# Gate-weight rounds of an mLSTM block moved from the end of the projections to their start, second slabs between first slabs, and another order of the modulation

## The chip, the cores and the metric

One NeuronCore of a Trainium2 chip. The metric is device time of one execution in microseconds. TensorE (PE) does matmuls, VectorE (DVE) and ScalarE (ACT) elementwise work, GpSimd (POOL) some more of it; SyncE (SP) issues all DMAs from one queue.

## The reference

One layer over 1024 latent tokens (width 1024) and 256 context tokens, all in fp32, cut to what matters:

```python
mod = silu(c) @ w_ada + b_ada                      # six sections of 1024: shift, scale, gate, twice
px = modulate(rms_norm(x, g_pre_mix), sh_m, sc_m) @ w_in     # and pc for the context with c_ctx
aq, ak, av, mq, mk, mv, mo, mg = split(px)         # attention q k v, mLSTM q k v o, 16 gate columns
att = window_attention(rope(aq), rope(ak), av, context keys and values, sink)   # 8 heads, 2 kv heads
mq, mk = silu(depthwise_conv3(mq, mk))
h = mlstm(mq, mk, mv, gates, forward) + mlstm(..., backward)   # state begun on the context
#   d[t,s] = b[t] - b[s] + i[s] for s <= t (backward: s >= t), else -inf;  b = cumsum(log_sigmoid(f))
#   weights exp(d - m_t) on the scores; decayed state added; divided by max(|den|, exp(-m_t))
ml = rms_norm(h) * g_mlstm_out * sigmoid(mo)
x = x + gt_m * rms_norm(concat(att, ml) @ w_out, g_post_mix)
x = x + gt_f * rms_norm(swiglu(modulate(rms_norm(x, g_pre_ffn), sh_f, sc_f)), g_post_ffn)
```

## The kernel before

Each fp32 product is made of three matmuls: operands are split in a high and a low part (`hh`, `hl` for tokens of the latent, `ch`, `cl` for the context; `w1h`, `w1l` and so on for weights), and high x high, high x low and low x high are summed in PSUM. Tokens go in tiles of 128: tiles 0 to 7 are latent, 8 and 9 context.

**The front.** The modulation comes in four quarters q (each two of eight blocks of the width): `pr_mm` multiplies by the weights, `mod_row` copies the row to SBUF, `mod_t` turns it into columns, and `mod_col` adds four partial sums and the bias. In the same quarters the first three tiles are projected as soon as a quarter is there (`sq(i, q)`, two PSUM slabs: the first of 272 columns with the 16 gates, attention values and one head of mLSTM values; the second of 384 columns with three more heads of values). `h_ts`, `h_hi`, `h_lo` modulate a tile's quarter and split it (DVE, ACT, DVE). `warm(n)` issues n matmuls on ones. Tiles 3 to 9 are prepared whole (`prep_c`: square and root on ACT, reciprocal on DVE, scaling on POOL; `prep_t`: transposes; `prep_m`, `prep_b`: modulation and split), and then get a first slab, `s1(i)`, and a second slab, `s2(i)`.

**Gates.** `gates()` needs all first slabs. It is a chain between DVE, ACT and PE: `pg` (cumulative sums), a running maximum, `pr`, a scan over chunks, `pm`, then `a_d` and `w_d` stored to DRAM, `pgt` transposed into `ucol`, and `pd`. Next, `ml_weights(n)` for each block n of 128 tokens makes the mLSTM's decay weights: for each direction d a broadcast load of `a_d` into a 128 x 512 buffer w (256 KB), four adds of a column of `ucol` and a mask (`mF` or `mB`) on DVE (L648), one exponential on ACT (L649), and a store of both directions to `w_dr[n]` (L650). I call one n a round.

**Projections.** The rest of the input projection is done by weight tiles, 13 of them (mk0 mk1 ak mq0 mq1 aq0 to aq3 mo0 to mo3), each against all tokens (`tproj`, L706 to L709); `tload` loads and splits the next weights. mk and mq go through `conv` (copies from PSUM, three DVE steps, Silu at L728). Between them lie `ada_rest` (the later sections of the modulation, on DVE), the state recursion of the mLSTM, and its queries. Of the rounds, 0 to 3 come right after the gates, 4 and 5 in mo0, 6 in mo1, 7 in mo2.

**Attention and mLSTM** follow as 16 items (block n, head group g): scores on PE (L880, L881), sums and minima on DVE (L882), exponentials on ACT (L891), scaling on POOL (L896), transposes (L1145), output (L1163). For each block the mLSTM loads the weights of its round from `w_dr` into `wl` (L903) and its queries into `qz` (L915; for blocks 0 and 1 POOL clears the tile first, L909), and PE multiplies them with state and values (L1061, L1065). The first two items' scores are already issued in mo3. `qz` of block 1 lies in buffer R8, which `ml_weights(4)` to `ml_weights(7)` use too.

The Tile scheduler sets each engine's order from its own estimates of when things are ready, except for instructions that are pinned (`pin`, the order of the program) or tied (`issue_after`). An engine works its instructions in order; SP's DMA issues too.

Of the kernel before, what the change touches and what calls it, by code (L numbers as in the profile page):

```python
# [16 lines left out]
P = 128  # L17
# [27 lines left out]
def body(tc, x, ctx, xtr, vecs, bcv, bada, gqm, gqf, wada, wmod, wsq, wt, wout, wfi, wfo,  # L45
# [134 lines left out]
    wraw = [vf[:, 1504 + 1312 * i:1504 + 1312 * (i + 1)] for i in range(2)]  # L180
# [49 lines left out]
    def prep_t(i, keep=False, parts=(0, 1)):  # L230

        xt = xts[i]
        if i >= XT:
            pts[i] = pa.tile([P, 4, P], F32, name="pt", tag="tp", bufs=2)[:, 0]
            pe.matmul(pts[i], st[:, 10 + i:11 + i].broadcast_to([P, P]), ident, start=True, stop=True)
            return
# [51 lines left out]
    def wq_load(q):  # L288
        return dma(wraw[q % 2], wsq[q])
# [17 lines left out]
    def mod_row(q):  # L307
        pin(act.copy(rr[:, 0:256], prs_[q][:, 0:256]))
        pin(dve.tensor_copy(rr[:, 256:512], prs_[q][:, 256:512]))

    pcl = {}

    def mod_t(q):
        pcl[q] = pa.tile([P, 4, P], F32, name=f"pcol{q}", tag="gx" if q < 1 else "tp", bufs=2)
        for k in range(4):
            pin(pe.transpose(pcl[q][:, k, :], rr[:, k * P:(k + 1) * P], ident))

    def mod_col(q):
# [4 lines left out]
        for g in range(4):  # L323
            pin(dve.tensor_tensor(o, pv_[:, g, :, 0:2], t, ADD))
            t = o
# [36 lines left out]
    def sq(i, q, mid=None):  # L362
# [9 lines left out]
        for n, (w, o, lo_) in enumerate(x_):  # L372
            if mid and n == 3:
# [8 lines left out]
    dve.tensor_scalar(bb[:, 1], bcol(1), 1.0, None, ADD)  # L382
    ld("x0 m00 m01 m02 m03 x1 w0 x2 m10 m11 m12 m13 w1")
# [23 lines left out]
    ld("w2")  # L407
# [51 lines left out]
    for i in (1, 2):  # L459
        h_ts(i, 2)  # L460
        h_hi(i, 2)
        h_lo(i, 2)
    pr_mm(3, 0)
    pr_mm(3, 1)
    prep_c(3, (0,))
    mod_row(3)
    prep_c(3, (1,))
    sq(1, 2, lambda: mod_t(3))
# [4 lines left out]
    h_hi(0, 3)  # L473
    w_lo(3, 0)
    h_lo(0, 3)
    w_lo(3, 1)
# [47 lines left out]
    def s2(i, bs=(0, 1)):  # L524

        if 0 in bs:
            s2ps[i] = pa.tile([P, 512], F32, name="slab", tag="mm", bufs=4)
        for b in bs:
            for k in range(4):
                mm3(s2ps[i][:, :384], hop(i, 4 * b + k), (w2h[b][:, k], w2l[b][:, k]), 4 * b + k == 0, 4 * b + k == 7)  # L530
        if 1 in bs:
            act.copy(vrow(i)[:, 1:4, 0:128], s2ps.pop(i)[:, 0:384].rearrange("p (h v) -> p h v", v=128))

# [6 lines left out]
    for i in range(ET):  # L540
        sqe = sq(i, 3)
# [5 lines left out]
        if i == 1:  # L547
# [15 lines left out]


    def gates():
# [11 lines left out]
        for d in range(2):  # L577
            f = G[:, 2 * d + 1].rearrange("p s h -> p (s h)")
            dve.scalar_tensor_tensor(lf[:, d * 64:d * 64 + 64], f, 0.0, tm[:, d * 64:d * 64 + 64], MIN, SUB)
        pg = pa.tile([P, 2, P], F32, name="pg", tag="gx", bufs=2)  # L580
        for d in range(2):
            r = slice(d * 64, d * 64 + 64)
            pe.matmul(pg[r, 0, :], lf[:, r], lw if d else up, start=True, stop=True)
            pe.matmul(pg[r, 1, :], G[:, 2 * d].rearrange("p s h -> p (s h)"), ident, start=True, stop=True)
# [12 lines left out]
        for i, t in enumerate((b, cm)):  # L597
            dve.tensor_copy(bl[0:64, i:i + 1], t[0:64, 127:128])
            dve.tensor_copy(bl[64:128, i:i + 1], t[64:128, 0:1])
        pr = pa.tile([1, 2, P], F32, name="pr", tag="gx", bufs=2)  # L600
        for i in range(2):
            pe.matmul(pr[0:1, i], bl[:, i:i + 1], ident, start=True, stop=True)
        pool.memset(mr, 0.0)
        dve.tensor_copy(rr.rearrange("p i d s h -> p i (d s h)"), pr)
        for d in range(2):
            for h in range(4):
                dve.tensor_tensor_scan(mr[:, d, 1:11, h], rr[:, 1, d, 0:10, h], rr[:, 0, d, 0:10, h], 0.0, MAX, ADD)
        pm = pa.tile([P, 1], F32, name="pm", tag="gx", bufs=2)
        pe.matmul(pm, mr.rearrange("p d s h -> p (d s h)"), one[0:1, 0:1], start=True, stop=True)
# [29 lines left out]

    def ml_weights(n):  # L640

        wt_ = R((6, 7, 8, 15)[n] if n < 4 else 8, f"w{n}", (2, 4, P))
        for d in range(2):
            s_, r0 = rows_of(n, d)
            w = wt_[:, d]
            dma(w, bcast(a_d[r0:r0 + 4, :].rearrange("(o h) t -> o (h t)", o=1)).rearrange("p (h t) -> p h t", h=4))
            for h in range(4):
                dve.scalar_tensor_tensor(w[:, h], w[:, h], ucol[:, r0 + h:r0 + h + 1], mB if d else mF, ADD, ADD)  # L648
            act.activation(w, w, AF.Exp)  # L649
# [1492 lines left out]
```

## Time and profile before

| | |
|---|---|
| median of 3 runs | 1198.51 us (1197.49 to 1199.38) |
| the profiled execution | 1199.53 us, span 1197.8 us |
| mean granted TensorE clock | 0.988 |
| TensorE busy | 1156.4 us, 97% of the span |
| VectorE, ScalarE, GpSimd busy | 776.5, 555.6, 152.0 us |

The page cuts the span into 40 slices of 30 us, and its PE row is in tenths of a slice:

```profile
PE   9989999997589999999999999999999999999997
PEclk9999999998889999999999999999999999999999
```

All slices but a few are full. The dip in slices 11 and 12 (counted from 1, 300 to 360 us, with the clock's 8s from 270 on) is where the projections hand over to attention.

### The profile page before, as it was taken

To read this page: it belongs to the slowest core of one execution; us is meant where nothing else is said; L and a number is where in the kernel's file an instruction comes from. 1 tells how busy PE (TensorE), PEld (TensorE's weight loads), DVE (VectorE), ACT (ScalarE), POOL (GpSimd) and SP (SyncE) were. 2 spreads that over 40 slices of the span, in tenths; PEclk is the share of its full clock that TensorE was granted. 3 is DMA by queue.
4 is the path that set the end of the run, shared out by engine and by line. 5 is a ranking of instruction groups with operands and counts; after the bars stand their busy time and mean duration, and the time that the engine had idled before them with its cause. 6 is when DMAs were issued, how large, how long until landed. Compare 5 with 4: busy or idle time off the path is not lost.

```text
span 1197.8 us, 16313 instructions
## 1 busy us (share of the span) xinstructions
PE 1156.4 (97%) x5901; PEld 952.3 (80%) x5901; DVE 776.5 (65%) x1417; ACT 555.6 (46%) x1035; POOL 152.0 (13%) x200
## 2 busy tenths in 40 slices
PE   9989999997589999999999999999999999999997
PEld 7889888786477876788788888888888888888886
DVE  4774758943766762458777678676777656544566
ACT  4553342223757883687534333333333435434443
POOL 1330012163335561000000000000000000000000
PEclk9999999998889999999999999999999999999999
DMA  9623736576749531421233565656543557665853
GB/s 373 256 71 94 301 106 211 160 219 204 222 145 277 177 77 58 172 87 71 62 123 132 202 219 202 213 218 237 202 167 124 197 184 260 202 216 188 298 195 123
DMA packets 102984, 216.99 MB, mean 181 GB/s; under 512 B 10228, under 2 KB 39540, under 8 KB 101496
## 3 DMA queue, kind: packets, MB, share of 16 engines
q1 hardware_dynamic: 102904, 215.95, 53.8%
q8 instruction: 46, 0.75, 0.3%
q14 instruction: 34, 0.28, 0.1%
HBM read 159.29 MB, written 55.97 MB: 180 GB/s over the span
## 4 chain that ended last, share of the span: by engine, by line
PE 82%; DVE 7%; DMA 4%; ACT 2%; SPq 2%; POOL 1%; issue 1%; DVEq 0%; ACTq 0%; POOLq 0%
PE xv L79 8%; PE xv L78 8%; PE xv L77 8%; PE pt L78 6%; PE pt L79 6%; PE pt L77 6%; PE pt L1163 2%; PE pt L1145 2%; PE op L79 2%; PE op L78 2%; PE op L77 2%; PE fx L77 2%; PE fx L79 2%; PE fx L78 2%; PE slab L378 2%; PE t L707 2%
## 5 line engine op out<-in xcount | busy, mean ns | idle before, releaser
L66 DVE TENSOR_TENSOR fo<-fr,fo 128x1024 fp32r<-128x1024 f32 x77 | 92.8, 1222 | 72.6 <-ACT fo L65 72.6
L65 ACT CAST fo<-fr 128x1024 fp32r<-128x1024 f32 x77 | 79.6, 1051 | 74.0 <-PE pt L79 34.8
L706 PE MATMUL t<-hh,th 128*128 128x512 f32 x208 | 82.3, 396 | 0.0
L707 PE MATMUL t<-hl,th 128*128 128x512 f32 x208 | 81.6, 392 | 0.0
L1545 ACT CAST wS<-wr 128x512 fp32r<-128x512 f32 x88 | 54.2, 623 | 55.2 <-PE pt L79 36.6
L1547 DVE TENSOR_TENSOR wS<-wr,wS 128x512 fp32r<-128x512 f32 x88 | 60.3, 688 | 19.8 <-ACT wS L1545 19.7
L77 PE MATMUL xv<-tT,wS 128*128 128x512 f32 x168 | 65.6, 390 | 0.0
L79 PE MATMUL xv<-tT,wS 128*128 128x512 f32 x168 | 65.6, 391 | 0.0
L78 PE MATMUL xv<-tT,wS 128*128 128x512 f32 x168 | 65.5, 390 | 0.0
L709 PE MATMUL t<-hh,tl 128*128 128x512 f32 x208 | 65.5, 394 | 0.0
L880 PE MATMUL s<-k,qh 128*128 128x256 f32 (+1 forms) x128 | 44.0, 352 | 10.3 <-DVE sm L882 7.5
L79 PE MATMUL op<-woh,ml 128*128 128x512 f32 x128 | 50.1, 391 | 1.3 <-DVE ml L66 1.3
L77 PE MATMUL op<-woh,mh 128*128 128x512 f32 x128 | 50.9, 398 | 0.0
L78 PE MATMUL op<-wol,mh 128*128 128x512 f32 x128 | 50.0, 390 | 0.0
L1293 DVE TENSOR_TENSOR wr<-wr 128x512 f32<-128x512 f32 x66 | 45.5, 690 | 1.4
L706 PEld LDWEIGHTS t<-hh,th 128*128 128x128 f32 x208 | 39.1, 188 | 8.3 <-issue 0.3
L707 PEld LDWEIGHTS t<-hl,th 128*128 128x128 f32 x208 | 39.1, 188 | 7.7 <-issue 0.7
L1579 ACT ACTIVATE es<-es 128x512 f32<-128x512 f32 x22 | 13.9, 633 | 66.5 <-DVE es L1296 66.5
L709 PEld LDWEIGHTS t<-hh,tl 128*128 128x128 f32 x208 | 37.4, 188 | 6.9 <-issue 0.7
L77 PE MATMUL pt<-fo 128*128 128x512 f32 x110 | 42.8, 389 | 0.0
L78 PE MATMUL pt<-fo 128*128 128x512 f32 x110 | 42.8, 389 | 0.0
L79 PE MATMUL pt<-fo 128*128 128x512 f32 x110 | 42.8, 389 | 0.0
(794 smaller groups left out, 3314.0 us busy)
## 6 DMA issues: line engine op xcount, KB each, us to landing
wr<-in_wfi SPq DMA_DIRECT2D x44, 512.0 KB, 4.7
wb<-in_wada SPq DMA_DIRECT2D x24, 512.0 KB, 5.9
s_d<-a SPq DMA_DIRECT2D x22, 512.0 KB, 6.5
bt<-in_wfo SPq DMA_DIRECT2D x44, 256.0 KB, 3.7
tb_d<-bt SPq DMA_DIRECT2D x11, 1024.0 KB, 3.9
fr<-s_d SPq DMA_DIRECT2D x44, 256.0 KB, 4.5
fr<-tb_d SPq DMA_DIRECT2D x44, 256.0 KB, 4.8
fr<-a_d SPq DMA_DIRECT2D x33, 256.0 KB, 4.5
```

Of the source, the lines that this page charges most:

```text
L65: act.copy(hi, raw)
L66: dve.tensor_tensor(lo, raw, hi.bitcast(F32), SUB)
L77: pe.matmul(ps, a[0], b[0], start=first, stop=False, **kw)
L78: pe.matmul(ps, a[0], b[1], start=False, stop=False, **kw)
L79: pe.matmul(ps, a[1], b[0], start=False, stop=last, **kw)
L706: pe.matmul(o, wh[:, kt], m[0], start=f, stop=False)
L707: pe.matmul(o, wh[:, kt], m[1], start=False, stop=False)
L709: pe.matmul(o, wl[:, kt], m[0], start=False, stop=l)
L880: pe.matmul(o, qh[:, h, :], k2[g][:, kc], start=True, stop=False)
L1293: dve.tensor_tensor(out, a, b, SUB)
L1545: act.copy(w[:, 0], raw)
L1547: dve.tensor_tensor(w[:, 1], raw, w[:, 0].bitcast(F32), SUB)
```

## The change

What it does:

- **Modulation.** Three raw weight buffers instead of two. For quarters 0 and 1 the four partial sums are added by a matmul with a selecting matrix (`sel2`) instead of transposes and three more adds. `mod_row` is one copy on ACT instead of halves on ACT and DVE. Loads are queued earlier, warming is 3 + 6 instead of 2 + 8, and steps of the quarters change places: `h_ts(0, 0)` ahead of the scaling of tile 1, the modulation of tile 3 behind the last quarter of tile 1.
- **Slabs.** All slab matmuls are pinned. Behind each first slab `s1(i)` from tile 3 to 8 stands half a second slab, with the transposes of tile i + 2. The activation table for exponential and logarithm is loaded ahead of the gates. The first projection weights are loaded one tile before the last.
- **Gates.** The chain is a generator, and its matmuls are pinned between pieces of the remaining second slabs: in the string of the diff, 605 is tile 6, k-tiles 0 to 5; g is the next step of the chain; t loads the second weights.
- **Rounds.** All eight rounds come right behind the gates, in eight buffer uses of R8, 15, 6, 4, 5, 7, 6, 5. For d = 1 in rounds 1, 3, 5, 6, 7 the mask is added by POOL over 128 x 512, and `ucol` goes in as the bias of four exponentials of 128 x 128 on ACT. The Silu in `conv` may issue only after the last exponential, and `ada_rest`'s first loads only after the last load of a round. In mo0 to mo2 no round is left.

```diff
-    wraw = [vf[:, 1504 + 1312 * i:1504 + 1312 * (i + 1)] for i in range(2)]
+    wraw = [vf[:, 192 + 1312 * i:192 + 1312 * (i + 1)] for i in range(3)]
+    sel2 = st[:, 52:54]
...
     def mod_row(q):
-        pin(act.copy(rr[:, 0:256], prs_[q][:, 0:256]))
-        pin(dve.tensor_copy(rr[:, 256:512], prs_[q][:, 256:512]))
+        pin(act.copy(rr, prs_[q]))
...
+    SUMQ = (0, 1)
...
         for k in range(4):
-            pin(pe.transpose(pcl[q][:, k, :], rr[:, k * P:(k + 1) * P], ident))
+            rk = rr[:, k * P:(k + 1) * P]
+            pin(pe.matmul(pcl[q][:, k, 0:2], rk, sel2, start=True, stop=True) if q in SUMQ else pe.transpose(pcl[q][:, k, :], rk, ident))
...
-        for g in range(4):
+        for g in range(1 if q in SUMQ else 4):
             pin(dve.tensor_tensor(o, pv_[:, g, :, 0:2], t, ADD))
...
-    warm(2)
+    warm(3)
     mod_t(0)
     prep_c(1, (0,))
     mod_col(0)
+    warm(6)
+    h_ts(0, 0)
     prep_c(1, (1,))
-    warm(8)
-    h_ts(0, 0)
...
-    ld("w2")
+    ld("w2 m30 m31 m32 m33 w3 x3 x4")
...
+    def pm3(ps, a, b, first, last):
+
+        for i, j in ((0, 0), (0, 1), (1, 0)):
+            pin(pe.matmul(ps, a[i], b[j], start=first and not i + j, stop=last and i == 1))
...
+        if i + 3 == NI:
+            pin(act.preload_act_table_set("natural_log_exp_and_others"))
         if i + 1 < NI:
             prep_b(i + 1)
-        with tc.issue_after(sqe) if i < ET + 2 else ExitStack():
-            s1(i)
-            if i < ET + 2:
-                s2(ET, (i - ET,))
+        s1(i)
+        if i < NI - 1:
+            s2(ET + (i - ET) // 2, range(4 * ((i - ET) % 2), 4 * ((i - ET) % 2) + 4))
+            if ET + 2 <= i + 2 < NI:
+                prep_t(i + 2, True)
...
+        if i == NI - 2:
+            tload(0)
...
+    wlast, elast = [None], [None]
+
     def ml_weights(n):
 
-        wt_ = R((6, 7, 8, 15)[n] if n < 4 else 8, f"w{n}", (2, 4, P))
+        wt_ = R((8, 15, 6, 4, 5, 7, 6, 5)[n], f"w{n}", (2, 4, P))
         for d in range(2):
             s_, r0 = rows_of(n, d)
             w = wt_[:, d]
-            dma(w, bcast(a_d[r0:r0 + 4, :].rearrange("(o h) t -> o (h t)", o=1)).rearrange("p (h t) -> p h t", h=4))
+            wlast[0] = dma(w, bcast(a_d[r0:r0 + 4, :].rearrange("(o h) t -> o (h t)", o=1)).rearrange("p (h t) -> p h t", h=4))
+            if d and n in (1, 3, 5, 6, 7):
+                pool.tensor_tensor(w, w, mB.rearrange("p (o t) -> p o t", o=1).broadcast_to([P, 4, P]), ADD)
+                for h in range(4):
+                    elast[0] = act.activation(w[:, h], w[:, h], AF.Exp, bias=ucol[:, r0 + h:r0 + h + 1]).ins
+                continue
             for h in range(4):
                 dve.scalar_tensor_tensor(w[:, h], w[:, h], ucol[:, r0 + h:r0 + h + 1], mB if d else mF, ADD, ADD)
-            act.activation(w, w, AF.Exp)
+            elast[0] = act.activation(w, w, AF.Exp).ins
         dma(w_dr[n], wt_.rearrange("p d h t -> p (d h t)"))
...
-    gates()
-    for i in range(NFILL, NI):
-        if i > ET:
-            s2(i)
-        if i in (NFILL + 1, NFILL + 2):
-            tload(i - NFILL - 1)
-        if NFILL < i < NFILL + 5:
-            ml_weights(i - NFILL - 1)
+    gt = gates()
+    next(gt)
+    for k in "605 g t 667 707 g 803 g 847 901 g 923 g 947".split():
+        if k == "g":
+            next(gt, None)
+        elif k == "t":
+            tload(1)
+        else:
+            s2(int(k[0]), range(int(k[1]), int(k[2]) + 1))
+    for n in range(NT):
+        ml_weights(n)
...
-            act.activation(d, t, AF.Silu)
+            with tc.issue_after(elast[0]):
+                act.activation(d, t, AF.Silu)
...
-        with tc.issue_after(twd[j].ins):
+        with tc.issue_after((twd[j] if acc_n.append(sec) or len(acc_n) > 1 else wlast[0]).ins):
...
-        for n in {"mo0": (4, 5), "mo1": (6,), "mo2": (7,)}.get(name, ()):
-            ml_weights(n)
```

How the order of the engines moves at three places. First the handover on DVE, where the first items' sums stand (`sm<-s`, the scores in PSUM). Before:

```order
L823 SCALAR_TENSOR_TENSOR cs_2539<-cs_2539,decb,pu 128x129 x4
L882 ISA pr__2690,sm<-s,mask,bcr 128x512
L882 ISA sm 128x1
L882 ISA pr__2690,sm<-s,mask,bcr 128x512
L882 ISA sm 128x1
L648 SCALAR_TENSOR_TENSOR w_2434<-w_2434,ucol,mF 128x128 x4
L648 SCALAR_TENSOR_TENSOR w_2434<-w_2434,ucol,mB 128x128 x4
L882 ISA pr__2690,sm<-s,mask,bcr 128x512
L882 ISA sm 128x1
```

And now:

```order
L846 SCALAR_TENSOR_TENSOR cs_2560<-cs_2560,decb,pu 128x129 x4
L905 ISA pr__2683,sm<-s,mask,bcr 128x512
L905 ISA sm 128x1
L905 ISA pr__2683,sm<-s,mask,bcr 128x512
L905 ISA sm 128x1
L905 ISA pr__2683,sm<-s,mask,bcr 128x512
L905 ISA sm 128x1
```

A round stood between the second and the third sum of item 0; the four sums now follow each other. Second, the handover on SP (`aq_dh`, `aq_dl` are the attention queries' two parts). Before:

```order
L650 DMA w_dr_980<-w_2562 128x1024
L920 DMA hs_2838<-so_d 128x4x128
L920 DMA hs_2977<-so_d 128x4x128
L903 DMA wl_3126<-w_dr_976 128x1024
L903 DMA wl_3290<-w_dr_977 128x1024
L646 DMA w_2659<-a_d 128x512 x2
L835 DMA qh<-aq_dh 64x4x128 x2
L835 DMA ql<-aq_dl 64x4x128 x2
L650 DMA w_dr_981<-w_2659 128x1024
L915 DMA qz_2968<-q_dr 64x2x128 x7
```

And now:

```order
L926 DMA wl_2672<-w_dr_1025 128x1024
L926 DMA wl_2959<-w_dr_1026 128x1024
L1010 DMA so_d<-so 128x1024
L938 DMA qz_2961<-q_dr 64x2x128 x4
L858 DMA qh<-aq_dh 64x4x128 x2
L858 DMA ql<-aq_dl 64x4x128 x2
L858 DMA qh<-aq_dh 64x4x128 x2
L858 DMA ql<-aq_dl 64x4x128 x2
L1133 DMA wor_3007<-in_wout 128x1024
L938 DMA qz_2674<-q_dr 64x2x128 x4
```

Before, the load of block 1's qz came in one piece behind the last round's store; now four of its loads stand ahead of the queries of later items, with no store of a round near them. Third, ACT where the first convolutions are (mk). Before:

```order
L649 ACTIVATE w_1207<-w_1207 128x512 x2
L65 CAST th_1391<-tw_1393 128x1024
L723 COPY cr<-t_0_1297 128x512
L723 COPY cr<-t_1_1298 128x512
L728 ACT_TABLE_LOAD
L728 ACTIVATE mk_1285<-ct 128x1024
```

And now:

```order
L65 CAST th_1440<-tw_1442 128x1024
L745 COPY cr<-t_0_1346 128x512
L745 COPY cr<-t_1_1347 128x512
L742 COPY cr<-tc_1348 128x256
L65 CAST th_1540<-tw_1542 128x1024
L677 ACTIVATE w_1294<-w_1294 128x512
L673 ACTIVATE w_1294<-w_1294,ucol 128x128 x4
L677 ACTIVATE w_1308<-w_1308 128x512
L673 ACTIVATE w_1308<-w_1308,ucol 128x128 x4
L751 ACT_TABLE_LOAD
L751 ACTIVATE mk_1334<-ct 128x1024
```

The exponentials of the last two rounds (`w_1294`, `w_1308`) stand between the copies of the first projection out of PSUM and its Silu.

More of the change, by code (lines that the diff above doesn't have):

```diff
@@ L234, in prep_t @@
             pts[i] = pa.tile([P, 4, P], F32, name="pt", tag="tp", bufs=2)[:, 0]
-            pe.matmul(pts[i], st[:, 10 + i:11 + i].broadcast_to([P, P]), ident, start=True, stop=True)
+            pin(pe.matmul(pts[i], st[:, 10 + i:11 + i].broadcast_to([P, P]), ident, start=True, stop=True))
             return
@@ L372, in sq @@
         for n, (w, o, lo_) in enumerate(x_):
-            if mid and n == 3:
+            if mid and n == at:
                 mid()
@@ L382, in body, with h_all @@
     dve.tensor_scalar(bb[:, 1], bcol(1), 1.0, None, ADD)
+    for k in range(1, 4):
+        dve.tensor_tensor(sel2, sel2 if k > 1 else ident[:, 0:2], ident[:, 32 * k:32 * k + 2], ADD)
+    def h_all(i, q):
+        h_ts(i, q)
+        h_hi(i, q)
+        h_lo(i, q)
     ld("x0 m00 m01 m02 m03 x1 w0 x2 m10 m11 m12 m13 w1")
@@ L458, in body @@
     sq(0, 2)
[L459 to L462, printed above, removed]
+    h_all(1, 2)
     pr_mm(3, 0)
+    h_all(2, 2)
     pr_mm(3, 1)
+    mod_row(3)
+    sq(1, 2, lambda: mod_t(3), 2)
     prep_c(3, (0,))
-    mod_row(3)
-    prep_c(3, (1,))
-    sq(1, 2, lambda: mod_t(3))
     w_hi(3, 0)
@@ L473, in body @@
     h_hi(0, 3)
+    prep_c(3, (1,))
     w_lo(3, 0)
+    w_lo(3, 1)
     h_lo(0, 3)
-    w_lo(3, 1)
     pool.memset(V[:, :, :, 128:129], 1.0)
@@ L522, in body, with s2, tload @@
     s2ps = {}
-    def s2(i, bs=(0, 1)):
-        if 0 in bs:
+    def s2(i, ks):
+        if 0 in ks:
             s2ps[i] = pa.tile([P, 512], F32, name="slab", tag="mm", bufs=4)
[L528 to L531, printed above, removed]
+        for k in ks:
+            pm3(s2ps[i][:, :384], hop(i, k), (w2h[k // 4][:, k % 4], w2l[k // 4][:, k % 4]), k == 0, k == 7)
+        if 7 in ks:
             act.copy(vrow(i)[:, 1:4, 0:128], s2ps.pop(i)[:, 0:384].rearrange("p (h v) -> p h v", v=128))
+    twd, tws = {}, {}
+    def tload(j):
+        wh = R(9 + j % 2, f"th{j}", (KT, P), F32R)
+        wl = R(11 + j % 2, f"tl{j}", (KT, P), F32R)
+        with tc.issue_after(xd[NI - 1].ins):
+            twd[j] = load_split(wh, wl, wt[j], R(13 + j % 2, f"tw{j}", (KT, P)))
+        tws[j] = wh, wl
     chain(lambda: dma(bcr, bcast(bcv)))
@@ L599, in gates @@
             dve.tensor_copy(bl[64:128, i:i + 1], t[64:128, 0:1])
+        yield
         pr = pa.tile([1, 2, P], F32, name="pr", tag="gx", bufs=2)
         for i in range(2):
-            pe.matmul(pr[0:1, i], bl[:, i:i + 1], ident, start=True, stop=True)
+            pin(pe.matmul(pr[0:1, i], bl[:, i:i + 1], ident, start=True, stop=True))
         pool.memset(mr, 0.0)
@@ L607, in gates @@
                 dve.tensor_tensor_scan(mr[:, d, 1:11, h], rr[:, 1, d, 0:10, h], rr[:, 0, d, 0:10, h], 0.0, MAX, ADD)
+        yield
         pm = pa.tile([P, 1], F32, name="pm", tag="gx", bufs=2)
-        pe.matmul(pm, mr.rearrange("p d s h -> p (d s h)"), one[0:1, 0:1], start=True, stop=True)
+        pin(pe.matmul(pm, mr.rearrange("p d s h -> p (d s h)"), one[0:1, 0:1], start=True, stop=True))
         mc, c1, dc = m[:, 0:1], m[:, 1:2], m[:, 2:3]
@@ L628, in gates @@
         dve.tensor_scalar(di, ind, dc, None, MUL)
+        yield
         pd = pa.tile([P, 64], F32, name="pd", tag="gx", bufs=2)
-        pe.matmul(pd, sel, di, start=True, stop=True)
+        pin(pe.matmul(pd, sel, di, start=True, stop=True))
         dve.tensor_copy(decb, pd)
```

59 lines of the change are left out of this document (22 added, 37 removed).

## The prediction

> **What bounds the kernel now.** I read the page first: the busy times and the chain that ended last.
>
> ```profile
> PE 1156.4 (97%) x5901; PEld 952.3 (80%) x5901; DVE 776.5 (65%) x1417; ACT 555.6 (46%) x1035; POOL 152.0 (13%) x200
> PE 82%; DVE 7%; DMA 4%; ACT 2%; SPq 2%; POOL 1%; issue 1%; DVEq 0%; ACTq 0%; POOLq 0%
> ```
>
> TensorE is the bound, and this change adds or removes hardly a matmul. So it can win only where PE stands still or runs slowly. I therefore took PE's waits over two stretches that the change touches: the handover from the projections to attention (285 to 345 us), and the front (0 to 112 us).
>
> ```profile
> PE pt L1061 <- DMA qz<-q_dr: 8.9, 1, 8.9
> PE s L880 <- DVE sm L882: 7.0, 4, 5.0
> PE s L880 <- DVE wl L1052: 2.6, 3, 1.9
> PE pt L1145 <- POOL pr__2854 L896: 2.1, 1, 2.1
> PE s L1047 <- ACT so L978: 1.9, 1, 1.9
> PE pt L1145 <- ACT ts__3021 L1150: 1.0, 1, 1.0
> PE pt L1061 <- ACT ts__2868 L1150: 0.7, 1, 0.7
> ...
> PE slab L378 <- ACT hh L355: 2.9, 3, 1.3
> PE pt L235 <- DVE st L220: 1.8, 2, 0.9
> PE slab L79 <- DVE hl L274: 0.9, 1, 0.9
> ```
>
> The columns are total, times and longest. The handover's seven add up to 24.2 us. Next, the windows (length, busy PE, PEld, DVE, ACT, POOL, granted clock, DMA share, GB/s):
>
> ```profile
> 120.00:180.00 60.00, 60.00 (x315) 50.50 (x314) 39.69 (x54) 22.84 (x34) 5.06 (x13) 1.00 0.54 202
> 285.00:300.00 15.00, 8.04 (x42) 6.98 (x40) 7.73 (x28) 6.73 (x17) 6.31 (x5) 0.66 0.66 183
> 300.00:320.00 20.00, 13.34 (x94) 11.13 (x93) 16.98 (x58) 17.55 (x37) 7.98 (x11) 0.99 0.82 244
> 320.00:340.00 20.00, 9.16 (x42) 6.50 (x41) 7.85 (x23) 8.60 (x18) 4.91 (x10) 0.58 0.38 110
> ```
>
> Between front and handover PE never rests (60.00 of 60.00), so what the front gains is carried to the handover unchanged, and nothing there can be gained by other engines. In the handover the clock falls to 0.66 and 0.58 in the windows that hold the two long gaps, and is 0.99 in the one between them. Third, the timeline at the handover:
>
> ```profile
> 285.71 0.61 PE L709 MATMUL t<-hh,tl 128*128 128x512 f32 x2
> 291.34 0.58 PE L880 MATMUL s<-k,qh 128*128 128x256 f32 x1 [5.01 <-DVE sm L882]
> 344.37 1.91 PE L1145 MATMUL pt<-vec,pr__2854 128*128 128x128 f32 x16
> 368.76 1.91 PE L1145 MATMUL pt<-vec,pr__3167 128*128 128x128 f32 x16
> ...
> 288.42 1.14 DVE L648 SCALAR_TENSOR_TENSOR w<-w,ucol,mF 128x128 f32<-128x128 f32 x4 [9.08 <-DMA w<-a_d]
> 327.70 0.33 SPq L650 DMA_DIRECT2D w_dr<-w  x1
> 330.32 11.09 SPq L915 DMA_DIRECT2D qz<-q_dr  x7
> 330.53 1.17 POOL L909 MEMSET qz<- 64x256 f32 x4 [4.97 <-DMA w_dr<-w]
> ```
>
> From the last projection matmul to item 2's transposes 58.7 us pass (344.37 - 285.71); from there to item 4's, two attention items in steady flow, 24.4 (368.76 - 344.37). The handover holds about two items' work too, so 34.3 us is the most that can be had here.
>
> **Part A, the weight rounds leave the handover.** Before, rounds 4 to 7 (load, eight adds on DVE, two exponentials, store) lie in mo0 to mo3 and all share one buffer, the one that qz of block 1 takes next. The rows name two victims. The softmax sums (L882) stand on DVE behind L648, which had sat 9.08 us for its loads: PE waits 5.01 for that. The last store goes out at 327.70; behind it wait the memset of qz (330.53, idle 4.97) and the qz loads (330.32): PE waits 8.9. Both causes are gone, since the rounds end some 150 us earlier. The 2.6 for wl I count as gone too: the weighted sums are late because DVE and the w_dr loads are. Together 5.0 + 8.9 + 2.6 = 16.5.
>
> The clock comes on top. The two slow windows hold those two gaps; at full clock their matmuls would take 8.04 x 0.66 = 5.3 and 9.16 x 0.58 = 5.3, which saves 2.7 + 3.8 = 6.5. So A gains 16.5 + 6.5 = 23.0. The other waits (2.1, 1.9, 1.0, 0.7 and 2.0 of the 7.0) are the start of a pipeline, scores to sums to exponentials to POOL, and I leave them. Ends: 13.9 if only the two long waits go and the freed time is spent at a slow clock; 34.3 if the handover becomes steady flow. I take 23.0, the sum of rows.
>
> The Trainium skill ("TensorE: Matmul & The Clock Gate", HAM clock gate) puts the fall to half clock at an idle window of about 3.4 us. By that rule no gap left over here (2.1 at most) would slow the clock, and A would be the same 23.0; but one new gap of that size would give part of the 6.5 back. The trace agrees as far as it goes: the gaps of 5.01 and 8.9 lie in slow windows, the window whose gaps are short has 0.99.
>
> **Part B, the front.**
>
> ```profile
> 13.54 0.57 DVE L324 TENSOR_TENSOR hs<-pcol,hs 128x8 f32<-128x8 f32 x3
> 14.34 1.41 DVE L352 TENSOR_SCALAR hraw<-hraw,hs 128x128 f32<-128x128 f32 x2
> 18.55 0.60 DVE L352 TENSOR_SCALAR hraw<-hraw,hs 128x128 f32<-128x128 f32 x2
> 44.52 1.28 DVE L259 TENSOR_TENSOR hraw<-pt,hs 128x512 f32<-128x512 f32 x2
> 45.29 2.04 POOL L270 TENSOR_TENSOR hraw<-hraw,hs 128x512 f32<-128x512 f32 x2 [0.41 <-DVE hraw L259]
> 45.79 1.62 DVE L352 TENSOR_SCALAR hraw<-hraw,hs 128x128 f32<-128x128 f32 x2
> ```
>
> First slab: three of the four adds of mod_col go (0.57), and the L352 pair, 1.41 while POOL scales the next tile and 0.60 at 18.55 with POOL idle, now runs ahead of POOL's work (0.8). That is 1.4, less the longer copy of the modulation row on ACT (a few tenths); only the slab's wait can shrink, so I take 1.1. Last first slabs: prep_m(3) (L259, 1.28) moves behind h_ts(1,3), and POOL's add (45.29), which made the pair 1.62 instead of 0.60, moves with it: 1.28 + 1.02 is more than the slab's whole wait of 1.3, so 1.3 goes. Later slabs: pt waits 1.8 and hl 0.9; a half of a second slab now stands behind each first slab, with prep_t behind it, so the preparation has cover; I take 2.0 of the 2.7. Bounds of B from above: all of 2.9 + 1.8 + 0.9 = 5.6.
>
> B's price is a new order on PE: the gate chain's matmuls are pinned between pieces of second slabs, so PE stops there if DVE is late, and all slabs and projections queue behind.
>
> ```profile
> 93.10 0.29 DVE L585 COPY g<-pg 128x128 f32<-128x128 f32 x1 [1.35 <-PE pg L584]
> 97.10 0.15 DVE L599 COPY g<-g 64x1 f32<-64x1 f32 x1
> 101.86 0.77 DVE L607 TENSOR_TENSOR_SCAN g<-g 1x10 f32<-1x10 f32 x8
> 112.02 0.34 PE L78 MATMUL slab<-w2l,ch 128*128 128x384 f32 x1
> 112.19 0.34 PE L79 MATMUL slab<-w2h,cl 128*128 128x384 f32 x1
> ```
>
> The matmuls of 384 columns follow each other by 0.17 (112.19 - 112.02). From pg to pr DVE needs 93.10 to 97.25, 4.2 plus hand-overs; 30 such matmuls (groups 667 and 707) cover it with 5.1. From pr to pm: one copy and eight scans (0.77), with hand-overs under 2; 12 matmuls cover 2.0. The covers are thin, some tenths each, so I charge 1.0 (up to 5 if DVE's conversion of the next tile or of th gets between). Net B: 1.1 + 1.3 + 2.0 - 1.0 = 3.4, ends -3 and 5.6.
>
> **Part C, all eight rounds at once.**
>
> ```profile
> 121.66 1.12 DVE L648 SCALAR_TENSOR_TENSOR w<-w,ucol,mB 128x128 f32<-128x128 f32 x4
> 140.10 1.06 ACT L728 ACTIVATE mk<-ct 128x1024 f32<-128x1024 f32 x1
> 144.98 1.06 ACT L723 COPY cr<-t 128x512 f32<-128x512 f32 x2
> 154.14 0.39 PE L706 MATMUL t<-hh,th 128*128 128x512 f32 x1
> ```
>
> DVE does 44 adds instead of 32 here: 12 x 0.28 = 3.4 us. POOL does five masks of 128x512; the row at 45.29 prices two of that form at 2.04, so 5.1 in all. ACT does three more whole exponentials and twenty of a quarter. The stretch 120 to 180 leaves DVE 20 us idle (60 - 39.69) and ACT 37, and PE is full, so I charge nothing. What falls due: the conv's Silu may issue only behind the last exponential. Before, it ran at 140.10; the copies that free the second projection's banks end at 146.0, 8.1 us before PE takes those banks again (154.14). The four rounds of before end on DVE at 122.8 (121.66 + 1.12); four more of the same are 4 x 2 x 1.12 = 9 us there, a few more with loads, so I estimate the last exponential near 135, inside that cover. Ends: 0, and 6 lost if the rounds end some 14 us later than that estimate. A gain is excluded, PE being full.
>
> On SP the eight moved loads and four moved stores now stand ahead of projection weights and of the first wada loads, which the change holds behind the last of them; DMA is busy 0.54 of that stretch, and PE has no wait there on a weight. The other edits (the third raw buffer and the earlier loads, the table preload, tload(0) one place earlier) touch what PE waits for in no row above: nothing, covered by the same full stretch; if a weight came late, PE would wait that long at once.
>
> A rule that speaks against this: "SBUF — State Buffer", SBUF: two separate sides, in the Trainium skill, says that GpSimd and VectorE share a port pair as an exclusive lock for a whole instruction. The trace agrees with a slowed L352 (1.41 and 1.62 against 0.60 beside POOL work). By it the masks would cost DVE up to the same 5.1 again, still less than its idle time, so the sum stands.
>
> **The sum.** 23.0 + 3.4 + 0 = 26.4 off the profiled execution's 1199.5, so 1173.1. The median shown, 1198.5, is 1.0 below that execution, so about 1172.
>
> **Rivals.**
> - The handover keeps a long gap. The loads of items 2's queries and of qz now queue on SP in one bunch, and ACT and POOL still start from nothing. Then only the low end of A comes, 13.9 + 3.4 = 17.3, and the time is 1181. For it: four of the seven waits do not name the rounds. Against it: the two longest do.
> - The early rounds hold the projections: bank copies late, or gate matmuls waited for. C costs 6: 26.4 - 6 = 20.4, so 1178. For it: ACT's queue holds ten exponentials between the first copies and the first Silu. Against it: 20 us of idle DVE.
> - The handover becomes nearly steady flow: A 33, B 3.4, so 1162. For it: the 34.3; against: the pipeline's start has to be paid once.
> - Slower: the same Silu gate, with the rounds so late (buffer reuse of rounds 6 and 7, or their loads behind each other in one queue) that mq0's banks are late by more than all gains. It decides from 26.4 us of stall on: the last exponential at about 135 + 14 + 26 = 175, forty late; at five more, 1203. Against it: four rounds end at 122.8 now.
>
> **How the numbers follow.** The sum 0.60 (own range 1167 to 1177), kept gap 0.16, held projections 0.12, steady flow 0.07, slower 0.03, and 0.02 for no visible change. 0.2% (2.4 us) is about what a measurement of this kernel can tell. The range runs from the middle of the steady-flow case to beyond the kept gap: 1162 to 1184. Faster 0.95, same 0.02, slower 0.03.
>
> **What would show it.** A: in the profile of after no L648 kind of add after 200 us, no PE wait over 4 us between the last projection and the transposes, granted clock over 0.9 there, and that stretch near 35 us, not 58.7. B: the first projection matmul some 3 us earlier than before, no new wait of a gate matmul over 1 us. C: PE full from the first projection to the handover. Wrong would be: a PE wait for t's banks between 120 and 180, or a new wait for qz or query loads of 5 us in the handover.

## The result, and the profile after

The changed kernel takes 1166.54 us (median of 4 runs, 1164.76 to 1169.29) against 1198.95 for the kernel before beside it: a ratio of 0.9732 (95% interval 0.9710 to 0.9755). In a later set of runs it was 1164.87 (ratio 0.9719, 0.9703 to 0.9735). Forecast was 1172 within 1162 to 1184; the gain is 32 us where 26.4 were worked out.

The page after: busy times, and the two rows by slices.

```profile
PE 1150.1 (99%) x5907; PEld 949.8 (82%) x5907; DVE 767.5 (66%) x1390; ACT 548.5 (47%) x1043; POOL 158.4 (14%) x205
PE   9999999999999999999999999999999999999997
PEclk9999999999999999999999999999999999999999
```

The dip (slices 10 to 12 before, with 7, 5 and 8 tenths) has gone, and PE does nearly the same work with 6 us less busy time: most of that was slow clock. The handover, and the stretch ahead of it, in the windows (length, busy PE, PEld, DVE, ACT, POOL, granted clock, DMA share, GB/s):

```profile
285.00:345.00 60.00, 59.57 (x455) 50.78 (x454) 47.61 (x164) 46.18 (x132) 36.53 (x41) 1.00 0.86 241
110.00:285.00 175.00, 172.53 (x914) 140.73 (x914) 123.68 (x205) 60.13 (x105) 48.90 (x75) 1.00 0.70 228
```

PE's waits from 285 to 345 us (total, times, longest):

```profile
PE pt L1166 <- ACT hs L1098: 0.4, 1, 0.4
```

And the timeline of PE:

```profile
287.25 0.62 PE L731 MATMUL t<-hh,tl 128*128 128x512 f32 x2
311.40 0.33 PE L1166 MATMUL pt<-vec,pr__2847 128*128 128x128 f32 x1
336.25 0.33 PE L1166 MATMUL pt<-vec,pr__3160 128*128 128x128 f32 x1
```

One wait of 0.4 us is left of seven waits and 24.2 us. From the last projection matmul (287.25) to item 2's transposes (311.40) 24.2 us pass, as many as two items take in steady flow behind them (336.25 - 311.40 = 24.9): the handover is steady flow from its first matmul. Before, it took 58.7, so it is 34.5 us shorter. What PE did in it, before and after:

```profile
285.71:344.37 58.66, 34.21 (x199) 27.49 (x198) 35.65 (x119) 34.42 (x76) 20.77 (x27) 0.77 0.59 169
287.25:311.40 24.15, 23.72 (x184) 19.71 (x182) 18.02 (x63) 17.89 (x47) 16.72 (x20) 1.00 0.77 218
```

Of the 34.5 us, 24.0 are idle time that went (58.66 - 34.21 against 24.15 - 23.72) and 10.5 are busy time. Of these 10.5 some 2 are no gain: 16 of the 56 score matmuls that stood in this stretch, ahead of item 2's transposes, now stand behind them (an estimate from their spacing, 0.17 and 0.12 us; behind the mark 1.8 us less idle time makes up for them). The remaining 8 or so are the slow clock. The spans differ by 32.9 (1197.8 and 1164.9), because the last projection matmul itself comes 1.5 us later than before (287.25 against 285.71). PE's waits between the gates and the handover (115 to 285 us), of which there were none before:

```profile
PE pu L838 <- DVE mkc L834: 2.0, 3, 1.1
PE t L728 <- ACT cr L745: 0.4, 1, 0.4
```

So nearly all of the time came from one place, and a little was given back on the way to it. The experiments ask which part of the change brought it, why all seven waits went and not three, and where the front's gain is.

### The profile page after: what moved, and what is told of

Same layout as the page of the kernel before. It is cut to its first block, busy times and chain, and to the rows that moved or that the text cites. A ratio compares the mean times of both kernels' runs of the same rounds, so it can differ in the third digit from the quotient of the medians.

```text
span 1164.9 us, 16332 instructions
## 1 busy us (share of the span) xinstructions
PE 1150.1 (99%) x5907; PEld 949.8 (82%) x5907; DVE 767.5 (66%) x1390; ACT 548.5 (47%) x1043; POOL 158.4 (14%) x205
## 4 chain that ended last, share of the span: by engine, by line
PE 84%; DVE 5%; DMA 4%; issue 2%; ACT 2%; POOL 1%; SPq 1%; DVEq 0%; ACTq 0%; POOLq 0%
PE xv L77 8%; PE xv L79 8%; PE xv L78 8%; PE pt L78 6%; PE pt L79 6%; PE pt L77 6%; PE slab L490 4%; PE pt L1184 3%; PE pt L1166 3%; PE op L77 3%; PE op L78 3%; PE op L79 3%; PE fx L77 2%; PE fx L78 2%; PE fx L79 2%
## 5 line engine op out<-in xcount | busy, mean ns | idle before, releaser
L731 PE MATMUL t<-hh,tl 128*128 128x512 f32 x208 | 65.8, 393 | 0.0
L77 PE MATMUL op<-woh,mh 128*128 128x512 f32 x128 | 50.9, 398 | 0.0
L903 PE MATMUL s<-k,qh 128*128 128x256 f32 (+1 forms) x128 | 41.6, 336 | 0.5 <-DVE sm L905 0.5
```

The lines of the kernel that those rows point to most:

```text
L77: pe.matmul(ps, a[0], b[0], start=first, stop=False, **kw)
L731: pe.matmul(o, wl[:, kt], m[0], start=False, stop=l)
```

## The experiments

The kernel before ran beside each set (1199.20, 1198.71, 1199.54 us). A single profile is no finer than some 2 us in its marks: the changed kernel, profiled a second time, had its last projection matmul at 285.15 instead of 287.25. Medians' ratios have intervals of some 0.0013 to 0.0023 to each side, 1.5 to 2.7 us.

### The rounds alone, and all but the rounds

The first kernel is the one before with only the rounds moved; the second the changed one with only rounds 4 to 7 put back.

```diff
 the kernel before:
-        wt_ = R((6, 7, 8, 15)[n] if n < 4 else 8, f"w{n}", (2, 4, P))
+        wt_ = R((8, 15, 6, 4, 5, 7, 6, 5)[n], f"w{n}", (2, 4, P))
...
+    for n in range(4, NT):
+        ml_weights(n)
     close(p1)
...
-        for n in {"mo0": (4, 5), "mo1": (6,), "mo2": (7,)}.get(name, ()):
-            ml_weights(n)
```

> The kernel before with one change: all eight weight rounds right behind the gates, in the eight buffer uses of the changed kernel, masks added on DVE as before; front, slabs and gate chain as before. Theory (late rounds held the handover): from the last projection matmul to item 2's transposes about 24 us instead of 58.7, no PE wait over 1 us there, clock 1.00; 34.5 off, at most 2.5 given back between the gates and the handover: 1165 to 1168 us. Rival (the new order of front, slabs and gates brings much of the gain): only the two long waits go, 1176 to 1185 us.

Measured: 1169.38 us, ratio 0.9751 (0.9737 to 0.9764). Item 2's transposes stand 24.2 us behind the last projection matmul (314.28 - 290.08), and the one PE wait there is 0.3 us. So the rounds alone carry 29.8 of the 32 us. The time was above the expected range by 1.4: that kernel's last projection matmul comes 4.4 us later than before (290.08 against 285.71), 2.1 of it waits for the state steps' `mkc`.

```diff
 the changed kernel:
-    for n in range(NT):
+    for n in range(4):
         ml_weights(n)
...
+        for n in {"mo0": (4, 5), "mo1": (6,), "mo2": (7,)}.get(name, ()):
+            ml_weights(n)
```

(Rounds 0 to 3 have their old buffers here, 4 to 7 share R8.)

> The changed kernel with rounds 4 to 7 put back into mo0 to mo2, all in buffer R8 as before; front, slabs, gate chain and the POOL masks as changed. Theory: the handover is as long as before (55 to 62 us to item 2's transposes, waits on qz and on the sums, clock under 0.85), and only the other parts' sum is left: front -2.3, slab stage +3.3, so 1195 to 1200 us. Rival: 1172 to 1190 us, since the other parts carry some of the gain.

Measured: 1204.95 us, ratio 1.0045 (1.0031 to 1.0059): slower than before. Nothing of the gain is in the other parts without this one. PE's waits of this kernel in the handover:

```profile
PE pt L1084 <- DMA qz<-q_dr: 11.1, 1, 11.1
PE s L903 <- DVE sm L905: 10.8, 3, 4.9
PE s L903 <- DVE sm L916: 5.2, 1, 5.2
PE s L1070 <- POOL pr__2683 L919: 1.5, 1, 1.5
PE pt L1084 <- ACT ts__2861 L1173: 0.9, 1, 0.9
```

And its window:

```profile
285.00:345.00 60.00, 31.26 (x166) 26.97 (x167) 29.19 (x95) 34.26 (x79) 22.81 (x28) 0.66 0.55 157
```

Here the last projection matmul comes 2.0 us earlier than before (283.69), and the handover takes 65.8 us (349.46 - 283.69) instead of 58.7. My expectation missed that: the rounds' new form (masks on POOL, four small exponentials for one) lies among the softmax's POOL and ACT work when the rounds are late, and makes the waits 29.5 us instead of 24.2. That the new form is the cause was not tried by itself.

### Why the late rounds took 34 us

The rounds were coded in mo0 to mo2, but in the trace of before they run in the handover. The rows are the last state steps on DVE, then loads and stores of rounds 4 to 7 on SP:

```profile
271.09 0.76 DVE L811 TENSOR_TENSOR mkc<-pk,wkcol 128x256 f32<-128x256 f32 x2 [3.76 <-PE pk L809]
...
280.40 1.45 SPq L646 DMA_DIRECT2D w<-a_d  x2
291.30 0.32 SPq L650 DMA_DIRECT2D w_dr<-w  x1
294.38 0.80 SPq L646 DMA_DIRECT2D w<-a_d  x2
301.50 0.33 SPq L650 DMA_DIRECT2D w_dr<-w  x1
304.87 0.80 SPq L646 DMA_DIRECT2D w<-a_d  x2
312.48 0.33 SPq L650 DMA_DIRECT2D w_dr<-w  x1
317.91 0.79 SPq L646 DMA_DIRECT2D w<-a_d  x2
327.70 0.33 SPq L650 DMA_DIRECT2D w_dr<-w  x1
```

R8 holds `mkc` until the last state step (written at 271.09). Then four rounds go through that one buffer, each loading only when the one ahead is stored: a chain of 10 to 15 us a link from 280 to 328, and qz of block 1 is its fifth link. SP works in order too, and stood 16.8 us ahead of the four stores, waiting for their exponentials, with later loads behind it:

```profile
SPq L650 <- ACT w L649: 16.8, 4, 7.0
```

Two experiments take links away. No run gave the late rounds buffers of their own in their old place, so what the shared buffer costs by itself, apart from the rounds being there at all, is not shown.

```diff
 the kernel before:
-                qz[n] = R((13, 8)[n], f"qz{n}", (2, 2, 2, P))
+                qz[n] = R((13, 15)[n], f"qz{n}", (2, 2, 2, P))
```

> The kernel before with one buffer changed: qz of block 1 in R15 (free after mo2's output gate) instead of R8, so that it doesn't wait for the last round's store. Theory (terms of the sum in the prediction): the 8.9 us wait and the slow clock behind it (3.8) go, the 5.0 us one stays: 1185 to 1188 us. Rival (the rounds that still stand in the handover's queues hold it anyway): 1192 to 1198 us, with a new wait of 4 us or more between 310 and 345 us.

Measured: 1190.07 us, ratio 0.9921 (0.9906 to 0.9937). PE's waits of this kernel in the handover:

```profile
PE s L880 <- DVE sm L882: 9.0, 1, 9.0
PE pt L1145 <- ACT hs L1077: 2.1, 1, 2.1
PE s L1047 <- ACT so L978: 1.9, 1, 1.9
```

The 8.9 us wait is gone and 8.6 us with it, less than the 12.7 expected: the other long wait grew from 5.0 to 9.0. What holds it stands on SP:

```profile
SPq L915 <- DMA so_d<-so: 7.4, 1, 7.4
```

The first loads of qz now stand on SP ahead of round 4's loads, and wait there 7.4 us until R15 is free (until `so` is stored), so that round 4 is loaded at 290.58 instead of 280.40. Nor did the 3.8 us for the clock come: PE's busy time is 1157.7 us against 1156.4, with a clock of 0.76 from 300 to 320 us, behind the longer wait. The time lies between the two expected ranges, nearer the first; a wait that is taken out of one queue went to the head of another.

```diff
 the kernel before, rounds 0 to 5 behind the gates in R8, 15, 6, 4, 5, 7:
-        for n in {"mo0": (4, 5), "mo1": (6,), "mo2": (7,)}.get(name, ()):
+        for n in {"mo0": (6,), "mo1": (7,)}.get(name, ()):
             ml_weights(n)
```

> The kernel before with rounds 0 to 5 behind the gates (as in the run with all eight there) and only 6 and 7 left late, in mo0 and mo1, both in R8. Theory (four rounds through one buffer are a chain of some 12 us each from the last state step on, 280 to 331 us; two end near 305, before qz of block 1 is wanted): most of the gain, item 2's transposes 26 to 32 us after the last projection matmul, 1170 to 1176 us. Rival (any round in the handover costs its wait on DVE, and that wait brings the slow clock): 1180 to 1190 us.

Measured: 1176.21 us, ratio 0.9811 (0.9796 to 0.9826), just above the chain's range. The chain ends at 300.65, the handover takes 33.4 us (320.07 - 286.72) where 26 to 32 were expected, and two waits of some size are left:

```profile
PE s L882 <- DVE sm L884: 3.4, 1, 3.4
PE s L1049 <- ACT so L980: 2.1, 1, 2.1
```

The rival's mechanism is there too, in small: behind the 3.4 us for DVE the clock falls, to 0.74 in the window from 285 to 300 us (this profile reads 0.95 where the others read 1.00, with matmuls as long as there).

Four late rounds cost 34.5 us in the handover, two cost about 9, none nothing. The waits that the prediction had put down to a pipeline's start (`sm` again, POOL's `pr`, `ts`: 7.7 us) shrink with the chain and vanish without it: with the softmax's sums on time the start is hidden behind the projections, where the first items' scores already are.

### The price of the early rounds

In the changed kernel the last exponential ended at 145.2 us, ten later than I had estimated. The rows on ACT:

```profile
143.95 1.29 ACT L673 ACTIVATE w<-w,ucol 128x128 f32<-128x128 f32 x4 [1.69 <-POOL w L671]
145.25 1.28 ACT L751 ACT_TABLE_LOAD   x1
146.55 1.06 ACT L751 ACTIVATE mk<-ct 128x1024 f32<-128x1024 f32 x1
151.28 0.42 ACT L751 ACTIVATE mkc<-ct 128x256 f32<-128x256 f32 x1 [3.67 <-DVE ct L749]
151.61 1.06 ACT L745 COPY cr<-t 128x512 f32<-128x512 f32 x2
```

The copies out of the second projection's banks (151.61) come just as PE wants them: it waited 0.4 us at 152.23. The cover of 8.1 us that the prediction counted was used up to its end. Two experiments change this place.

```diff
 the changed kernel:
-            if d and n in (1, 3, 5, 6, 7):
+            if False:
```

> The changed kernel with all masks and columns added on DVE and one exponential for each half round, as before; nothing of the rounds on POOL. Theory (PE is full there, DVE has some 20 us idle; 20 more adds of 0.28 are 5.7 us): the same within 1.5 us, 1165 to 1168 us, and the last exponential not later than now (145 us), since POOL's masks took 1.3 to 2.8 us each. Rival (DVE becomes late): waits of PE for the second projection's banks of 2 to 5 us near 152 us, 1169 to 1172 us.

Measured: 1167.05 us, ratio 0.9735 (0.9720 to 0.9749): no difference from the changed kernel. The last exponential starts at 142.94 instead of 143.95. PE has no wait near 152 us, but one of 2.7 us for DVE (`aq`, L766) at 236.78 that the changed kernel's two profiles lack. So the masks on POOL bring and cost nothing that the time shows.

```diff
 the changed kernel:
-            with tc.issue_after(elast[0]):
-                act.activation(d, t, AF.Silu)
+            act.activation(d, t, AF.Silu)
```

> The changed kernel with the conv's Silu no longer tied to the last exponential; everything else as changed. Theory (ACT's copies that free the second projection's banks are a wall at 152 us, because they stand behind the last exponential at 145 us and the first conv's Silu): the Silu of mk0 near 140 us, no PE wait on those copies; by itself that frees only the 0.4 us that PE waits there now, so 0 to 1 us faster in the same pairing: 1165 to 1167 us. Rival (the two more table loads on ACT and the moved conv delay the rounds' stores or the state steps): 1168 to 1171 us.

Measured: 1164.14 us, ratio 0.9708 (0.9692 to 0.9725), against 0.9719 (0.9703 to 0.9735) for the changed kernel in the same set. The Silu comes at 135.74 instead of 146.55, two more table loads of 1.28 us stand on ACT, and PE has no wait on those copies. As expected, this by itself can't be told from no change.

> The changed kernel unaltered, on the chip of these runs, as the measure for the other three: 1166.5 us within 1.5 us, PE wait of 0.4 us near 152 us and of 1.7 us near 253 us as in its first profile.

Measured: 1164.87 us, as above, just under the expected range; in that profile the 152 us wait was absent, and the state steps' wait was 1.6 us.

### The front

The last of the first three tiles' slab matmuls starts at 54.4 us after and at 52.2 before: the new front is not ahead, as forecast, but behind. (Three profiles with the front and slabs of before have 51.8 to 52.3, five with the new front 53.8 to 54.6.) Its wait from 22 to 30 us:

```profile
PE slab L380 <- ACT hh L357: 1.0, 1, 1.0
```

And the window behind it:

```profile
25.00:30.00 5.00, 4.79 (x26) 4.79 (x27) 3.71 (x10) 2.39 (x6) 0.00 (x0) 0.72 1.03 410
```

A wait of 1.0 us, and behind it the clock falls to 0.72. Three kernels ask whether that matters.

```diff
 the changed kernel:
-    SUMQ = (0, 1)
+    SUMQ = ()
```

> The changed kernel with the modulation's quarters 0 and 1 transposed and added on DVE as before (no 128x2 sum matmuls). Theory (the 128x2 matmuls of quarter 1 keep the array nearly idle behind a 1.0 us wait, and so the clock falls to 0.72 at 25 to 30 us): clock back at 1.00 there, 1.7 us of slow clock saved against 0.6 us of adds per quarter, so 0 to 2 us faster than the changed kernel: 1164.5 to 1166.5 us. Rival (the wait alone brings the slow clock): clock still under 0.85 at 25 to 30 us and 0.5 to 1.5 us slower: 1167 to 1168 us.

Measured: 1169.14 us, ratio 0.9752 (0.9739 to 0.9765): above both expected ranges, and slower than the changed kernel by 2 to 4 us (the interval overlaps that of the first set, not that of the later one), not faster. The theory of the clock was right in this window and wrong on the time. The same window of this kernel:

```profile
25.00:30.00 5.00, 4.42 (x28) 3.77 (x28) 4.01 (x13) 2.13 (x5) 0.00 (x0) 1.00 1.03 409
```

The clock is whole, but the adds are back on DVE (another wait of 0.6 us at 27.9), and at 50.9 PE waits 1.75 us for POOL's scaling of the next tile, which the changed kernel doesn't. The last of these slab matmuls starts at 55.1, and the wait for the second projection's banks is 1.9 us.

```diff
 the changed kernel, parts of the edit:
     def mod_row(q):
-        pin(act.copy(rr, prs_[q]))
+        pin(act.copy(rr[:, 0:256], prs_[q][:, 0:256]))
+        pin(dve.tensor_copy(rr[:, 256:512], prs_[q][:, 256:512]))
...
-    SUMQ = (0, 1)
+    SUMQ = ()
...
-    sq(2, 0, lambda: mod_t(1), 1)
-    mod_col(1)
+    sq(2, 0)
     h_ts(0, 1)
     h_hi(0, 1)
+    t_cp(2, 1, act)
...
```

> The changed kernel with the front of before (order of the modulation's quarters, transposes and four adds, halves of the row, warming, places of the loads); slabs, gate chain and rounds as changed. Theory (the new front loses time, the slab stage gains): the last of the first three tiles' slab matmuls at 52.2 us instead of 54.4, all of it kept: 1163.5 to 1165.5 us. Rival (the early marks are no loss, since the new front does work that the old one leaves for later): the same as the changed kernel or slower, 1166 to 1169 us.

Measured: 1167.86 us, ratio 0.9743 (0.9729 to 0.9758): the rival's range. The last slab matmul of the first tiles starts at 52.8, yet PE then waits 1.8 us at 151.76 for the banks, and the last projection matmul is at 287.30, where the changed kernel's first profile had it (287.25).

```diff
 the changed kernel:
-    sq(0, 0, lambda: prep_t(1, True))
+    sq(0, 0, lambda: prep_t(1, True), 4)
...
     pr_mm(1, 1)
-    mod_row(1)
     h_hi(2, 0)
+    mod_row(1)
...
     sq(2, 2)
-    prep_t(3, True)
...
         if not i:
+            prep_t(3, True)
             prep_b(3)
```

> The changed kernel with three steps of its front moved: tile 3's transposes behind the last quarter of tile 0 (PE waited 1.55 us for POOL there), tile 2's high part ahead of the modulation row on ACT (1.04 us), tile 1's transposes behind one more slab pair (0.48 us). Theory: these three waits, 3.1 us, go, about 2.5 is kept: 1163 to 1165 us. Rival (others take their place, the modulation's own chain above all): last slab matmul of the first tiles still near 54 us, 1165.5 to 1167.5 us.

Measured: 1165.31 us, ratio 0.9723 (0.9706 to 0.9740). The wait at 17 us goes, the one at 25 shrinks to 0.4, and the clock stays whole at 25 to 30 us. In place of the 1.55 us for POOL at 47.5, though, PE waits 0.4 and 1.5 us for DVE (`hraw`, L260), so the rival is in part right. The last slab matmul of the first tiles starts at 52.8; but again PE waits at 151.93 for the banks, now 2.0 us. PE's waits from 115 to 285 us in this kernel:

```profile
PE t L728 <- ACT cr L745: 2.0, 1, 2.0
PE pu L838 <- DVE mkc L834: 1.7, 2, 1.1
```

So there was a wall near 152 us, but not at a fixed time. In the six profiles of kernels with all rounds early and the tie, the copies start 7.0 to 7.7 us behind the start of the last exponential (151.61 - 143.95 in the changed kernel), whatever the front did, and the copies' start lies between 149.72 and 153.51. PE's wait depends on both sides: it is 1.8 and 2.0 us in the two kernels whose front is ahead, but also 1.9 with `SUMQ = ()`, whose front is behind (copies at 153.51), and nothing in the second profile of the changed kernel (copies at 149.72). That an earlier front makes PE wait as much longer is therefore not shown.

> The two edits together: the three moved steps of the front and the Silu no longer tied. Theory of the wall: the front's 1.6 us (last slab matmul of the first tiles at 52.8 instead of 54.4) now reach the handover, since the 2.0 us wait near 152 us is gone: 1163 to 1165 us, 1.5 to 3 us faster than the changed kernel. Rival (another wait behind it takes the time, the state steps' near 253 us above all): 1165 to 1167 us.

This is the last diff and that of the untied Silu together. Measured: 1165.32 us, ratio 0.9723 (0.9704 to 0.9743). PE's waits of this kernel from 115 to 285 us:

```profile
PE pu L837 <- DVE mkc L833: 1.3, 2, 0.8
```

In its profile the wait at the wall is gone, the last slab matmul of the first tiles starts at 52.46 and the last projection matmul is at 283.30, 1.9 us ahead of the changed kernel beside it; in the median nothing of it is seen. In all three kernels without the tie PE has no wait there; that removing it is worth anything in time is not shown.

> The front of before with the changed slabs, gates and rounds, and the Silu no longer tied. Theory of the wall: its wait of 1.8 us near 152 us is gone, so that it is 1 to 2 us faster than the same kernel with the tie (1167.9): 1165.5 to 1167 us. Rival: the same 1167 to 1169 us.

The old front with the untied Silu: 1166.51 us, ratio 0.9735 (0.9712 to 0.9757), PE's wait near 152 us gone, last projection matmul at 284.21; against 0.9743 with the tie no difference that can be told.

None of the variants is clearly faster than the changed kernel: the interval of the lowest median, 1164.14 (untied Silu), overlaps that of the changed kernel.

## Why the prediction was right, and where it was off

- **Direction, place and range: right.** The gain is that of part A; with rounds 4 to 7 back in place nothing of it is left, and with the rounds alone 29.8 of the 32 us are there.
- **Part A, 23.0 forecast, 34.5 found.** This is the mis-sized term. The step that failed is "the other waits are the start of a pipeline, and I leave them". They were not a start that has to be paid, but the same lateness further on: DVE late with the sums, POOL and ACT behind it. The waits were sized at 16.5 us, and 24.0 us of idle time went; the clock was sized at 6.5, and some 8 went. The rest, about 2, is score work on the other side of the mark. The upper end, 34.3, that the prediction had from comparing with steady flow, met the 34.5 in part by that luck; it was still much nearer than the sum over waits that name the rounds, which was too narrow. The rival that named it ("nearly steady flow", 0.07) was given too little.
- **The total came nearer than its largest term by luck in part.** A was 11.5 us short, the total only 6, because C, put at nothing, took some back.
- **The 8.9 and the 5.0 as terms of their own** do not add as the prediction had them: with qz in its own buffer the first vanished and the second grew by 4.0.
- **The clock, 6.5 forecast:** PE's busy time over the whole kernel fell by 6.3 (1156.4 to 1150.1) for the same work, slow clock at the new front counted in. That is in line with the forecast, but the reading behind it, that each long gap brings its slow window, holds for the first gap only. Before the 8.9 us gap the clock had fallen already:

```profile
317.40 0.44 PE L880 MATMUL s<-k,qh 128*128 128x384 f32 x1 [1.04 <-DVE sm L882]
319.25 0.47 PE L880 MATMUL s<-k,qh 128*128 128x384 f32 x1 [0.33 <-DVE sm L882]
319.00:320.00 1.00, 0.74 (x3) 0.75 (x4) 0.28 (x3) 1.00 (x1) 0.63 (x1) 0.77 0.95 334
320.00:321.00 1.00, 0.48 (x3) 0.18 (x1) 0.16 (x1) 0.97 (x3) 0.94 (x2) 0.50 0.90 322
```

It falls to 0.50 between 319 and 320 us, behind waits of 1.04 us and less, and the 8.9 us gap starts only near 324.
- **Part B, net 3.4 forecast:** its steps failed at the front, its sum about held. The first slab did start sooner (15.56 against 16.24), but POOL's scaling of tile 3, placed later (44.74 against 40.85) and beside DVE work (2.72 us against 1.13), made PE wait 1.55 us at 47.5, and the clock fell at 25 us: the first tiles' last slab matmul starts 2.3 us later. The slab stage more than makes up for it: the waits of 60 to 80 us (3.2) are all gone, and no gate matmul waits. In time, B is the changed kernel against the rounds alone: 1169.4 against 1166.5 and 1164.9, by the ratios some 2 to 4 us, at the edge of what the intervals tell apart. When the front itself is put back, no difference is seen. The sign "first projection matmul some 3 us earlier" can't be read, since the context's part of that projection now stands among the slabs (from 87.94 instead of 112.36).
- **Part C, 0 forecast:** it cost some. PE stood 2.4 us between the gates and the handover in the changed kernel and 2.1 with the rounds alone, where it had not stood before. One of the prediction's signs of being wrong, a wait for t's banks between 120 and 180, was there in small. The place of the held-projections rival was right (banks, 0 to 2.0 us), and so was its direction; its price of 6 was too high. The larger part is the state steps' wait for DVE, which no rival named. The trace of after shows its way:

```profile
242.69 1.72 POOL L871 TENSOR_TENSOR qb<-qb,mq 128x128 f32<-128x128 f32 x4 [13.00 <-DVE aq L763]
244.37 2.37 POOL L765 TENSOR_TENSOR rb<-rb,sint 128x1024 f32<-128x1024 f32 x1
246.77 1.23 DVE L766 TENSOR_TENSOR aq<-aq,rb 128x1024 f32<-128x1024 f32 x1 [2.93 <-POOL rb L765]
252.51 0.41 DVE L834 TENSOR_TENSOR mkc<-pk,wkcol 128x256 f32<-128x256 f32 x1
```

POOL now multiplies `qb` ahead of the rotation's `rb`; before, `rb` ran first, at 238.26. DVE waits 2.93 us for it, and `mkc`, behind it in DVE's order, comes late for PE. The rounds-alone kernel has the same order on POOL (245.94 and 247.61). Putting `rb` first again was not tried.
- **The masks.** After, one of them stands on POOL beside sixteen adds on DVE:

```profile
122.27 4.37 POOL L671 TENSOR_TENSOR w<-w,mB 128x512 f32<-128x512 f32 x1 [2.19 <-DMA w<-a_d]
121.19 3.23 DVE L676 SCALAR_TENSOR_TENSOR w<-w,ucol,mF 128x128 f32<-128x128 f32 x12
124.34 1.13 DVE L676 SCALAR_TENSOR_TENSOR w<-w,ucol,mB 128x128 f32<-128x128 f32 x4
```

Here POOL lost, not DVE: the mask took 4.37 us where the last two took 1.29 and 1.28, and it ended 1.2 us behind the last of the adds (126.64 against 125.47), which kept their 0.27 each. The Trainium skill ("SBUF — State Buffer", SBUF: two separate sides) says that whichever engine starts first holds the shared pair and the other blocks. The rows agree with a lock, and show that a run of short instructions on DVE can hold a long one on POOL to its end; the 5 us that I had allowed on DVE did not come.

## What to carry to other kernels

Where several waits of different names stand together behind a change of stages, compare the stretch with the same work in steady flow before adding up the waits by name: that difference is what one cause can be worth, if the marks on both sides have the same work between them. Ask of work that is coded early but runs late which buffer it waits for; here four rounds through one buffer, handed on from the state steps to a fifth user, cost 34 us at the worst place. And look for the chain that sets a place further on (here the copies out of a bank, 7 to 8 us behind the start of the last exponential) before polishing what lies ahead of it: part of such a gain can become waiting there.

## What the runs showed of the hardware that I had not expected

The clock fell without a long gap, in the kernel before at 319 us (above) and in the changed kernel's front. At 25 us the changed kernel's PE stood 1.0 us and then did a modulation quarter as eight matmuls of 128x2 (0.8 us from 25.57 to 26.37); the window's clock was 0.72, and in four other profiles with the same two things 0.75, 0.66, 0.76 and 0.66. With the wait but transposes instead of the 128x2 matmuls it was 1.00, and with the 128x2 matmuls but a wait of 0.4 us 1.00 too (two profiles). The Trainium skill ("TensorE: Matmul & The Clock Gate", HAM clock gate) names an idle window of about 3.4 us for the fall. The 5.0 us wait before is longer than that, though the clock (0.91 in the window from 288 to 289 us, 0.50 behind it) fell some 2.5 us into it. The fall at 25 us fits only if matmuls of two columns count as nearly idle, and even then the stretch, from 24.17 to 26.37, is under 3 us; ahead of the fall at 319 us the longest wait in 5 us is 1.04. What exactly counts was not tried.
